# Storing the last two result tiles whole instead of in halves and quarters

## The chip, the cores and the metric

One core of a Trainium2 chip runs the program. The metric is the device time of one execution in microseconds (us), as the median over executions. A profile gives one execution in detail; its span is some 2 us shorter than that execution's time. "Tile" here is 64 of the 1024 matrices of the result, 1 MB (1,049 KB); there are 16, numbered 0 to 15, and the change concerns tiles 14 and 15.

## The reference

```python
a = np.random.randn(1024, 64, 64).astype(np.float32)
b = np.random.randn(1024, 64, 64).astype(np.float32)
return np.matmul(a, b).astype(np.float32)
```

33.5 MB are read and 16.8 MB written.

## The kernel before

The engines are named as in the profile: PE multiplies matrices, DVE and ACT are the vector and the scalar engine, POOL is the general one, and SP here issues transfers and waits for them. SBUF and PSUM are memories on the chip; the transfers themselves run on 16 DMA engines, fed by queues.

For each tile, `a` is transposed and spread into block-diagonal weights, `b` is cast to bf16, the matmuls fill PSUM, and ACT and DVE copy ("evacuate") the result into an SBUF tile `o_sb`. From there POOL's DMA queue stores it. The parts that matter:

```python
o_v = out.rearrange("(t gh x) (mo w) n -> t (x mo) gh (w n)", gh=8, x=8, w=4)
...
    o_sb = o_pool.tile([128, 8, 2, 2, 64], fp32, name="o_sb")

    def put(lo, n):                      # store n of the 8 parts, from lo on
        nc.gpsimd.dma_start(
            out=o_v[t, :, lo : lo + n, :],
            in_=o_sb[:, lo : lo + n].rearrange("p gh j wl n -> p (gh j wl n)"),
        )
...  # matmuls and evacuations; the last tile is evacuated in quarters, by ACT and DVE in turn
    if last:
        held[t] = [lambda q=q: put(2 * q, 2) for q in range(4)]
    else:
        whole = t < n_t - 2
        held[t] = [lambda q=q: put(q, 8 if whole else 4) for q in ([0] if whole else [0, 4])]
...
for t in range(n_t):
    ...
    multiply(t)
    ...
    if t >= HOLD - 1:                    # HOLD = 2: the store of t is issued after multiply(t + 1)
        store(t - HOLD + 1)
for t in range(n_t - HOLD + 1, n_t):
    store(t)
```

Each partition holds 8 KB of a tile, and by `o_v` they go to eight pieces of 1 KB in the output, 128 KB apart (`gh` steps over 8 matrices of 16 KB). A store waits only for the copies that fill its part of `o_sb`, so a half or quarter can be issued before the tile is complete. That is what the pieces are for.

Of the kernel before, what the change touches and what calls it, by code (L numbers as in the profile page):

```python
# [13 lines left out]
def kernel(  # L14
# [19 lines left out]
    n_t, n_s = B // 64, B // 128  # L34
# [27 lines left out]
    held = {}  # L62
# [90 lines left out]
    def multiply(t):  # L153
        at_bd = bd_tiles[t % N_BD][:].rearrange("p j g wl h mo -> p j g (wl h mo)")
        at_bd = at_bd.bitcast(bf16).rearrange("p j g (c u) -> p j g c u", u=2)
        b_bf = bbf_tiles.pop(t)
        last = t == n_t - 1
        o_sb = o_pool.tile([128, 8, 2, 2, 64], fp32, name="o_sb")

        def put(lo, n):  # L160
# [5 lines that stand above are left out]
        def evacuate(o_ps, gh, n, copies):  # L166

            for par in range(2):
                for wl in range(2):
                    src = o_ps[64 * wl : 64 * wl + 64, :, par, :, :]  # L170
                    dst = o_sb[64 * par : 64 * par + 64, gh : gh + n, :, wl, :]
                    copies[2 * par + wl](dst, src)  # L172

        for half in range(2):
            if not last:
                o_ps = o_psum.tile([128, 4, 2, 2, 64], fp32, name="o_ps")
            for g8 in range(8):
                if last and g8 % 4 == 0:
                    o_ps = t_psum.tile([128, 2, 2, 2, 64], fp32, name="at_ps")
                g = 8 * half + g8  # L180
                gl = (g8 % 4 if last else g8) // 2
                for j in range(2):
                    for u in range(2):
                        nc.tensor.matmul(  # L184
                            o_ps[:, gl, g % 2, j, :],
                            at_bd[:, j, g, :, u],
                            b_bf[:, g, 64 * u : 64 * u + 64],
                            start=(u == 0),
                            stop=(u == 1),
                        )  # L190
                if last and g8 % 4 == 3:
                    copy = nc.scalar.copy if g8 == 3 else nc.vector.tensor_copy
                    evacuate(o_ps, g // 4 * 2, 2, [copy] * 4)
            if not last:
                copies = [nc.scalar.copy] * 4
                if half and t % 2:
                    copies[2:] = [nc.vector.tensor_copy] * 2
                evacuate(o_ps, 4 * half, 4, copies)
        if last:
            held[t] = [lambda q=q: put(2 * q, 2) for q in range(4)]  # L200
        else:
            whole = t < n_t - 2
            held[t] = [lambda q=q: put(q, 8 if whole else 4) for q in ([0] if whole else [0, 4])]

    with tc.manual_schedule():
        load_first_a()
# [18 lines left out]
        for t in range(n_t):  # L225
            s, half = t // 2, t % 2
            if t + 1 < n_t:
                spread(t + 1)
                cast(t + 1)
            if t + B_AHEAD < n_t:  # L230
                load_b(t + B_AHEAD)
            if half == 0 and 0 < s < n_s - 1 - A_AHEAD:
                load_a(s + 1 + A_AHEAD)
            if half == 0 and 0 < s < n_s - 1:
                transpose(s + 1, 1)
            multiply(t)
            if t == 0:
                regroup(1)
                load_a(A_AHEAD)
                load_a(A_AHEAD + 1)  # L240
                transpose(1, 0)
                transpose(1, 1)
            elif t == 1:
                regroup(2)
            elif half == 0 and s + 2 < n_s:
                regroup(s + 2)
            if half == 1 and s + 2 < n_s:
                transpose(s + 2, 0)
            if t >= HOLD - 1:
                store(t - HOLD + 1)  # L250
# [32 lines left out]
```

## Time and profile before

| | before |
|---|---|
| time, median of 3 | 135.43 us (135.34 to 135.49) |
| profiled span | 133.8 us |
| last result copy ends | 121.4 us |
| last store issued / landed | 122.4 / 132.3 us |

The result stores on the page, by size (count, KB each, median us from issue to landing):

```profile
out_dram<-o_sb POOLq DMA_DIRECT2D x14, 1024.0 KB, 23.6
out_dram<-o_sb POOLq DMA_DIRECT2D x2, 512.0 KB, 11.4
out_dram<-o_sb POOLq DMA_DIRECT2D x4, 256.0 KB, 10.1
```

At the end the time to landing hardly depends on the size: a quarter tile takes 10.1 us, a half 11.4, and tile 13, stored whole, 12.7. (The 23.6 us of the whole tiles is a median over the entire kernel.) Such a time is mostly waiting in the queue.

### The profile page before, as it was taken

How to read it: one execution, taken by the hardware profiler on the slowest of the kernel's cores; microseconds unless marked ns; L12 is line 12 of the kernel's file. 1: busy time of each engine (PE TensorE's matmuls, PEld its weight loads, DVE VectorE, ACT ScalarE, POOL GpSimd, SP SyncE). 2: the span in 40 equal slices, each digit the busy share in tenths (PEclk: the TensorE clock that was granted, in tenths of full speed). 3: DMA queues.
4: the chain of work that ended last, by engine and by line, in shares of the span. 5: the costliest groups of instructions: out<-in, count | busy, mean ns of one | idle time of the engine just before them, and what ended most of it. 6: DMA issues, size and time to landing. Idle time of an engine off the chain costs nothing.

```text
span 133.8 us, 2832 instructions
## 1 busy us (share of the span) xinstructions
PE 65.7 (49%) x1152; PEld 62.7 (47%) x1152; DVE 94.6 (71%) x120; ACT 87.7 (66%) x161; POOL 38.5 (29%) x49
## 2 busy tenths in 40 slices
PE   0007307970077463749919744991876376640000
PEld 0007207970077353649909744991866266630000
DVE  5930499108997059999999999899959989992000
ACT  3225424998038996758998985899793987992000
POOL 8991000420091080334124042003301220637000
PEclk9999999999559999555996896589677775797555
DMA  3999999999999999999999999999999999999991
GB/s 75 376 331 311 306 315 311 307 301 309 306 307 382 366 312 309 388 397 397 317 304 352 399 392 377 314 307 364 398 385 391 392 401 398 404 388 353 338 334 42
DMA packets 17485, 45.01 MB, mean 336 GB/s; under 512 B 1088, under 2 KB 1088, under 8 KB 17472
## 3 DMA queue, kind: packets, MB, share of 16 engines
q0 software_dynamic: 7440, 22.28, 54.8%
q1 hardware_dynamic: 5520, 13.11, 27.0%
q10 hardware_dynamic: 4512, 9.44, 18.6%
q8 instruction: 9, 0.15, 0.4%
q14 instruction: 4, 0.03, 0.1%
HBM read 33.55 MB, written 16.78 MB: 376 GB/s over the span
## 4 chain that ended last, share of the span: by engine, by line
DMA 35%; SPq 27%; DVE 15%; issue 6%; ACT 3%; POOL 3%; PE 3%; POOLq 1%; DVEq 0%; ACTq 0%
SPq L72 22%; DMA a_raw<-in_a_dram 18%; DMA b_sb<-in_b_dram 17%; DVE at_bd L128 8%; DVE b_bf L139 5%; SPq L91 3%; POOL out_dram L161 3%; PE o_ps L184 3%; ACT o_sb L172 2%; DVE o_sb L172 1%; SPq L85 1%; ACT b_bf L146 1%; DVE a_bf L106 1%; DVE a_bf L103 1%; POOLq L278 1%
## 5 line engine op out<-in xcount | busy, mean ns | idle before, releaser
L172 ACT COPY o_sb<-o_ps 64x512 f32<-64x512 f32 x106 | 61.6, 581 | 14.3 <-PE o_ps L184 13.0
L184 PEld LDWEIGHTS <-at_bd 128*128 128x128 bf16 x1024 | 41.6, 111 | 34.9 <-DVE b_bf L139 22.4
L184 PE MATMUL o_ps<-b_bf,at_bd 128*128 128x64 bf16 x960 | 41.9, 215 | 31.1 <-DVE b_bf L139 20.9
L128 DVE COPY at_bd<-at_sb 32x1024 f32<-32x1024 f32 x64 | 46.0, 719 | 13.4 <-ACT at_sb L118 11.6
L161 POOL DMA_DIRECT2D out_dram<-o_sb x20 | 20.6, 1031 | 58.1 <-ACT o_sb L172 21.4
L115 PE MATMUL at_ps<-identity,a_bf 128*128 128x128 f32 x128 | 23.4, 360 | 20.6 <-ACT a_bf L100 11.0
L115 PEld LDWEIGHTS at_ps<-identity,a_bf 128*128 128x128 f32 x128 | 21.6, 196 | 20.8 <-issue 19.3
L118 ACT COPY at_sb<-at_ps 128x512 f32<-128x512 f32 x32 | 16.9, 596 | 8.2 <-PE at_ps L115 8.0
L68 POOL DMA_DIRECT2D a_sb<-in_a_dram x21 | 13.9, 673 | 25.9 <-DVE a_bf L103 19.9
L139 DVE CAST b_bf<-b_sb 128x2048 bf16<-128x2048 f32 x14 | 17.4, 1245 | 2.9 <-DMA b_sb<-in_b_dram 2.6
L172 DVE COPY o_sb<-o_ps 64x512 f32<-64x512 f32 x14 | 9.7, 690 | 0.6 <-ACT o_sb L172 0.3
L106 DVE CAST a_bf<-a_raw 128x1024 bf16<-128x1024 f32 x7 | 5.5, 792 | 5.7 <-DMA a_raw<-in_a_dram 5.7
L103 DVE COPY a_bf<-a_sb 128x3072 bf16<-128x3072 bf16 x7 | 7.0, 1006 | 0.0
L100 ACT CAST a_bf<-o_sb 128x1024 bf16<-128x1024 f32 x2 | 2.1, 1044 | 5.0 <-DMA o_sb<-in_a_dram 5.0
L139 ACT CAST b_bf<-b_sb 128x2048 bf16<-128x2048 f32 x1 | 1.9, 1898 | 3.8 <-DMA b_sb<-in_b_dram 3.8
L100 DVE CAST a_bf<-o_sb 128x1024 bf16<-128x1024 f32 x2 | 2.8, 1380 | 1.9 <-DMA o_sb<-in_a_dram 1.9
L212 DVE MEMSET at_bd<- 128x4096 f32 x1 | 3.5, 3472 | 0.8 <-issue 0.8
L172 DVE COPY o_sb<-at_ps 64x256 f32<-64x256 f32 x8 | 3.4, 422 | 0.3 <-PE at_ps L184 0.2
L172 ACT COPY o_sb<-at_ps 64x256 f32<-64x256 f32 x8 | 2.9, 367 | 0.1
L209 ACT ACT_TABLE_LOAD x1 | 1.3, 1283 | 2.3 <-issue 2.3
L184 PE MATMUL at_ps<-b_bf,at_bd 128*128 128x64 bf16 x64 | 2.0, 193 | 1.2 <-DVE at_bd L128 1.2
L217 POOL MEMSET at_bd<- 128x2048 f32 x1 | 1.8, 1849 | 0.0
(12 smaller groups left out, 5.5 us busy)
## 6 DMA issues: line engine op xcount, KB each, us to landing
out_dram<-o_sb POOLq DMA_DIRECT2D x14, 1024.0 KB, 23.6
a_sb<-in_a_dram POOLq DMA_DIRECT2D x21, 256.0 KB, 17.4
a_raw<-in_a_dram SPq DMA_DIRECT2D x7, 512.0 KB, 24.2
o_sb<-in_a_dram ACTq DMA_DIRECT2D x2, 512.0 KB, 7.0
o_sb<-in_a_dram SPq DMA_DIRECT2D x2, 512.0 KB, 5.9
out_dram<-o_sb POOLq DMA_DIRECT2D x2, 512.0 KB, 11.4
out_dram<-o_sb POOLq DMA_DIRECT2D x4, 256.0 KB, 10.1
b_sb<-in_b_dram SPq DMA_DIRECT2D x8, 0.5 KB, 22.2
```

Of the source, the lines that this page charges most:

```text
L68: nc.gpsimd.dma_start(out=a_sb[:, h, :, :].rearrange("p v k -> p (v k)"), in_=a_v[s, h])
L72: nc.sync.dma_start(out=a_raw[:].rearrange("p v k -> p (v k)"), in_=a_v[s, 3])
L100: copy(a_bf[:, :, h, :], a_sb[h].rearrange("p (v k) -> p v k", v=16))
L103: nc.vector.tensor_copy(a_bf[:, :, 0:3, :], cast_sb[:].rearrange("p h v k -> p v h k"))
L106: nc.vector.tensor_copy(a_bf[:, :, 3, :], raw[:])
L115: nc.tensor.transpose(at_ps[:, vo, :], a_cols[:, 4 * vo + 2 * j + wl, :], identity[:])
L118: nc.scalar.copy(at_tiles[s][:, j, :, wl, :, :], at_ps[:].rearrange("p vo (g mp) -> p g mp vo", mp=4),)
L128: nc.vector.tensor_copy(bd[rows, :, :, :, h, :].rearrange("p j g wl mo -> p j (g wl) mo"), at_tiles[t // 2][rows, :, half, :, :, :].rearrange(
L139: (nc.vector.tensor_copy if t else nc.scalar.copy)(b_bf[:], b_sb[:])
L161: nc.gpsimd.dma_start(out=o_v[t, :, lo : lo + n, :], in_=o_sb[:, lo : lo + n].rearrange("p gh j wl n -> p (gh j wl n)"),)
L172: copies[2 * par + wl](dst, src)
L184: nc.tensor.matmul(o_ps[:, gl, g % 2, j, :], at_bd[:, j, g, :, u], b_bf[:, g, 64 * u : 64 * u + 64], start=(u == 0), stop=(u == 1),)
```

## The change

It makes the code simpler: one store for every tile, four DMA issues fewer. The whole diff:

```diff
-        if last:
-            held[t] = [lambda q=q: put(2 * q, 2) for q in range(4)]
-        else:
-            whole = t < n_t - 2
-            held[t] = [lambda q=q: put(q, 8 if whole else 4) for q in ([0] if whole else [0, 4])]
+        held[t] = [lambda: put(0, 8)]
```

## The prediction

> **What bounds the kernel now.** The change touches only the last two result tiles, so the question is what sets the end of the span. I read the page's DMA rows first, then a table of windows over the end, then every result store with its landing, then the last instructions in order of time, and last who waits in the DMA queue's own sequencer (SP).
>
> The page's 40 slices (3.34 us each), for DMA share and for GB/s:
>
> ```profile
> DMA  3999999999999999999999999999999999999991
> GB/s 75 376 331 311 306 315 311 307 301 309 306 307 382 366 312 309 388 397 397 317 304 352 399 392 377 314 307 364 398 385 391 392 401 398 404 388 353 338 334 42
> ```
>
> Apart from the first and last slice the DMA engines are never under nine tenths busy, while on the same page the busiest compute engine, DVE, has 71% of the span. The transfers are the bound: first loads and stores together, at the end stores alone. The windows over the end (after the window's length come busy time and count for PE, PEld, DVE, ACT and POOL, then PE clock, DMA share, GB/s):
>
> ```profile
> 115.00:118.00 3.00, 1.83 (x59) 1.67 (x57) 2.72 (x5) 2.93 (x6) 1.10 (x2) 0.93 1.03 406
> 118.00:121.60 3.60, 0.49 (x17) 0.37 (x13) 2.97 (x8) 3.25 (x9) 2.18 (x3) 1.00 1.01 366
> 121.60:125.00 3.40, 0.00 (x0) 0.00 (x0) 0.00 (x0) 0.00 (x0) 1.42 (x2) 0.59 1.01 349
> 125.00:128.00 3.00, 0.00 (x0) 0.00 (x0) 0.00 (x0) 0.00 (x0) 0.00 (x0) 0.50 1.02 347
> 128.00:130.00 2.00, 0.00 (x0) 0.00 (x0) 0.00 (x0) 0.00 (x0) 0.00 (x0) 0.50 0.96 338
> 130.00:131.00 1.00, 0.00 (x0) 0.00 (x0) 0.00 (x0) 0.00 (x0) 0.00 (x0) 0.50 0.56 213
> 131.00:132.00 1.00, 0.00 (x0) 0.00 (x0) 0.00 (x0) 0.00 (x0) 0.00 (x0) 0.50 0.10 41
> ```
>
> Compute is over by 121.6 us; the DMA engines stay full until 130 us. So some 8 us of finished, queued stores drain after the last result copy. The last engine instructions, in order of time (start, length, engine, line, operation, count, idle before and its releaser):
>
> ```profile
> 116.23 0.92 POOL L161 DMA_DIRECT2D out_dram<-o_sb  x1 [1.05 <-ACT o_sb L172]
> ...
> 117.59 3.49 DVE L172 COPY o_sb<-at_ps 64x256 f32<-64x256 f32 x8 [0.22 <-PE at_ps L184]
> 118.34 3.03 ACT L172 COPY o_sb<-at_ps 64x256 f32<-64x256 f32 x8
> 118.61 0.75 POOL L161 DMA_DIRECT2D out_dram<-o_sb  x1 [1.46 <-ACT o_sb L172]
> 120.14 2.96 POOL L161 DMA_DIRECT2D out_dram<-o_sb  x4 [0.77 <-ACT o_sb L172]
> ```
>
> These are the six issues that the change replaces: tile 14 in halves at 116.23 and 118.61, tile 15 in quarters from 120.14 to 123.10. The reader should not take the end of the chain of waits (123.1 us) for the end of the kernel: that chain follows instructions, and 10.7 us of the span come after it. What they are is in the SP waits:
>
> ```profile
> SPq L278 <- DMA out_dram<-o_sb: 41.8, 3, 40.8
> ```
>
> SP sits at the program's last line until the result stores have landed. The end is therefore the landing of the last store plus the closing (the span ends at 133.8).
>
> The stores looked at one by one (issue start plus time to landing): tile 12 is issued at 108.71 and lands 15.2 us later, at 123.9; tile 13 at 113.83, 12.7 later, 126.5; the halves of tile 14 at 116.23 + 11.9 = 128.1 and 118.61 + 11.0 = 129.6; the quarters of tile 15 at 120.14 + 10.2 = 130.3, about 131.0, 121.67 + 10.0 = 131.7 and 122.38 + 9.9 = 132.3. Ten microseconds from issue to landing for 256 KB is queueing, not transfer.
>
> **What the Trainium skill says.** (1) "Perfetto Trace Analysis", section on the per-instruction lifecycle: the data movement of a DMA falls outside the reported window of its instruction. The trace agrees: a quarter's issue shows 0.71 us, its landing is 10 us away; so I use landings. (2) "DMA: Bandwidth & Descriptors", "Queues, rings and completion order": on each DMA engine descriptors are consumed in ring order. The section says it of the SP and ACT queues; for the POOL queue the landings above, in order of issue, agree. (3) The same page, "Measured (HBM→SBUF, 128 partitions, SWDGE, issued from GpSimd)": 64 KB reach 138 GB/s and 1 MB 341 GB/s, and it advises to batch to 1 MiB. That would make quarters poor. The trace does not agree for queued stores: the quarters land about 0.65 us apart, (132.3 - 130.3) / 3 = 0.67, which is 262 KB / 0.67 us = 390 GB/s. (4) The same page, "Anatomy of one DMA — SWDGE (gpsimd) path": about 2 us fixed per DMA, mostly completion latency. The 0.67 us between landings shows that it overlaps with the next transfer here.
>
> **The change part by part.** Nothing else moves: the order of instructions on PE, DVE, ACT and SP is unchanged, and POOL has 45 rows instead of 49.
>
> Tile 14. Removed: an issue of 0.92 us and one of 0.75 us. Added: one whole issue; the whole ones just before took 0.90 and 1.35 us. Moved: the first half (0.52 MB) is offered at 118.6 instead of 116.2, 2.4 us later, since the store must now wait for the last ACT copy of the tile, which already released the second half. Is this on the path? What is still to be moved at 118.6 is the sum of rate times length of the windows: 3.0 x 366 + 3.4 x 349 + 3 x 347 + 2 x 338 + 213 + 41 = 1098 + 1187 + 1041 + 676 + 254 = 4256 KB, and a tile is 1049 KB: 4.06 tiles, that is tiles 12 to 15 entire. Ahead of tile 14 lie two tiles, 2.1 MB, or 2.1 MB / 355 GB/s = 5.9 us of work. The issue takes at most 1.35 us. The delay is hidden with over 4 us to spare: cost 0.
>
> Tile 15. Removed: four issues, 2.96 us from 120.14 to 123.10. Added: one of 0.9 to 1.35 us, which can start when the last copy ends: ACT at 118.34 + 3.03 = 121.37 (DVE at 121.08), plus the 0.3 us seen between copy and issue (118.32 to 118.61), so 121.65, done by 122.6 to 123.0. The first quarter is offered 1.5 us later, the last no later than before. Still to be moved at 121.6: 4256 - 1098 = 3158 KB = 3.01 tiles, so tiles 13 and 14 lie ahead of it, some 6 us. Cost 0.
>
> The end. The same bytes go through the same 16 engines, which have no gap. Four completions fewer per engine: at 0.67 us a quarter against 1049 KB / 347 GB/s = 3.0 us a tile, a quarter of which is 0.76, I see no surcharge to win back; I put 0.1 us on it. Sum: 0 + 0 - 0.1 us, 135.43 to about 135.3.
>
> **The rivals.** (a) The delay shows. If my reading of the backlog is wrong, the worst is a tile 15 that finds the queues empty: 121.65 + 1.35 issue + 3.0 transfer + about 2 us of completion (the skill's figure, an estimate) = 128.0, still 4.3 us before today's last landing of 132.3. So even a wrong backlog does not lengthen the kernel by this way; only a slower transfer of whole tiles would. (b) Engine imbalance. The drop from full to empty takes 130 to 132 us, so engines differ by some 2 us; the leading ones reach tile 14 and 15 earlier than the mean. 5.9 us of work less 2 is still more than the delay, and an idle leader would not lengthen the laggard. (c) A gain: the rate falls from 406 GB/s before 118 us to about 347 after it, near the time at which halves and quarters are first queued. If small stores cause this, whole ones could move 11 us at 400 instead of 347: 11 x (1 - 347/400) = 1.5 us saved, 134.0 us. Against it: by the landings, what moves from 118 to 126 is mostly tiles 12 and 13, which are whole already. I give it about one in ten. (d) POOL: it is 29% busy, its last issue ends about where it did, and nothing else waits for it; no bound.
>
> **Range and chances.** The three runs before span 0.15 us, so noise is small. The middle is 135.3. Half of rival (c) gives about 134.5 as the low end; 0.6 us for something in the tail that I can't see gives 135.9. A change of 2% is 2.7 us, nearly twice the whole gain of (c) and, for a loss, as much as nearly a whole tile's transfer. Faster by over 2%: 0.02; within 2%: 0.96; slower: 0.02.
>
> **What would show it.** In the changed profile: one issue for tile 14 at about 118.6 and one for tile 15 at about 121.65; DMA share near 1 in every window until 130; landings of tile 14 near 129.6 and tile 15 near 132.2; compute ending unchanged at 121.4. Rival (c) would show as GB/s staying near 400 between 118 and 128 and the last landing near 131. I am wrong if a window between 118 and 129 shows a DMA share well under 1 (starved engines), or if whole tiles take clearly over 3 us each to land at the end.

## The result, and the profile after

The kernel after takes 135.44 us (median of 4, 135.23 to 135.56), beside 135.38 us for the kernel before on the same chip. The ratio is 1.0001, with a 95% interval of 0.9984 to 1.0019. Ratios here and below are the mean time of one kernel's runs over that of the other's of the same rounds, so not quite the ratio of the medians quoted.

The two DMA rows of its page hardly differ from those before (40 slices; DMA share in tenths, then GB/s):

```profile
DMA  3999999999999999999999999999999999999991
GB/s 72 373 330 309 309 315 311 308 303 305 307 307 379 371 297 316 391 394 398 315 308 351 403 384 379 314 309 361 395 391 389 393 398 398 408 388 361 343 340 69
```

The windows over the end, in the same columns as in the prediction:

```profile
115.00:118.00 3.00, 1.58 (x52) 1.46 (x50) 2.54 (x5) 2.94 (x6) 0.63 (x1) 0.99 1.02 403
118.00:121.60 3.60, 0.94 (x33) 0.82 (x29) 3.38 (x8) 3.48 (x10) 0.89 (x1) 1.00 1.04 378
121.60:125.00 3.40, 0.00 (x0) 0.00 (x0) 0.00 (x0) 0.06 (x1) 0.89 (x1) 0.54 1.00 345
125.00:128.00 3.00, 0.00 (x0) 0.00 (x0) 0.00 (x0) 0.00 (x0) 0.00 (x0) 0.50 1.01 345
128.00:130.00 2.00, 0.00 (x0) 0.00 (x0) 0.00 (x0) 0.00 (x0) 0.00 (x0) 0.50 0.95 338
```

The DMA share stays near 1 up to 130 us although the stores come later. The rate falls from 403 to 345 GB/s just as before, now with no small store in the queue. The last instructions in order of time:

```profile
118.05 3.47 DVE L172 COPY o_sb<-at_ps 64x256 f32<-64x256 f32 x8 [0.41 <-PE at_ps L184]
118.65 3.01 ACT L172 COPY o_sb<-at_ps 64x256 f32<-64x256 f32 x8
118.92 0.89 POOL L161 DMA_DIRECT2D out_dram<-o_sb  x1 [3.29 <-ACT o_sb L172]
122.06 0.89 POOL L161 DMA_DIRECT2D out_dram<-o_sb  x1 [2.26 <-ACT o_sb L172]
```

Two issues stand where six stood. Tile 14 is offered whole at 118.92 and takes 10.5 us to land, at 129.4; tile 15 at 122.06, and takes 10.1, landing at 132.1 to 132.2. Before, the last halves and quarters landed at 129.6 and 132.3.

### The profile page after: what moved, and what is told of

It reads as the page before. It is cut to its first block, busy times and chain, and to the rows that moved or that the text cites. A ratio compares the mean times of both kernels' runs of the same rounds, so it can differ in the third digit from the quotient of the medians.

```text
span 133.4 us, 2824 instructions
## 1 busy us (share of the span) xinstructions
PE 64.3 (48%) x1152; PEld 60.6 (45%) x1152; DVE 94.9 (71%) x120; ACT 87.7 (66%) x161; POOL 35.6 (27%) x45
## 4 chain that ended last, share of the span: by engine, by line
DMA 34%; DVE 19%; SPq 16%; ACT 9%; PE 7%; issue 6%; POOLq 1%; ACTq 1%; DVEq 0%
DMA b_sb<-in_b_dram 34%; SPq L72 13%; DVE at_bd L128 8%; ACT o_sb L172 7%; DVE o_sb L172 5%; PE o_ps L184 3%; DVE b_bf L139 3%; PE at_ps L115 3%; SPq L91 2%; ACT at_sb L118 2%; DVE a_bf L106 1%; DVE a_bf L103 1%; SPq L85 1%; PE at_ps L184 1%; POOLq L274 1%
## 5 line engine op out<-in xcount | busy, mean ns | idle before, releaser
L184 PEld LDWEIGHTS <-at_bd 128*128 128x128 bf16 x1024 | 40.3, 110 | 37.6 <-DVE b_bf L139 23.6
L184 PE MATMUL o_ps<-b_bf,at_bd 128*128 128x64 bf16 x960 | 40.6, 212 | 32.8 <-DVE b_bf L139 20.8
L161 POOL DMA_DIRECT2D out_dram<-o_sb x16 | 18.5, 1155 | 60.5 <-ACT o_sb L172 24.8
L115 PE MATMUL at_ps<-identity,a_bf 128*128 128x128 f32 x128 | 22.9, 354 | 20.4 <-ACT a_bf L100 11.2
L115 PEld LDWEIGHTS at_ps<-identity,a_bf 128*128 128x128 f32 x128 | 20.7, 189 | 20.6 <-issue 19.9
L68 POOL DMA_DIRECT2D a_sb<-in_a_dram x21 | 13.0, 634 | 26.2 <-DVE a_bf L103 19.7
L106 DVE CAST a_bf<-a_raw 128x1024 bf16<-128x1024 f32 x7 | 6.3, 907 | 5.7 <-DMA a_raw<-in_a_dram 5.7
```

What stands on the lines that cost most here:

```text
L68: nc.gpsimd.dma_start(out=a_sb[:, h, :, :].rearrange("p v k -> p (v k)"), in_=a_v[s, h])
L106: nc.vector.tensor_copy(a_bf[:, :, 3, :], raw[:])
L115: nc.tensor.transpose(at_ps[:, vo, :], a_cols[:, 4 * vo + 2 * j + wl, :], identity[:])
L161: nc.gpsimd.dma_start(out=o_v[t, :, lo : lo + n, :], in_=o_sb[:, lo : lo + n].rearrange("p gh j wl n -> p (gh j wl n)"),)
L184: nc.tensor.matmul(o_ps[:, gl, g % 2, j, :], at_bd[:, j, g, :, u], b_bf[:, g, 64 * u : 64 * u + 64], start=(u == 0), stop=(u == 1),)
```

## The experiments

The theory: two tiles of queued stores lie ahead of each of the last two, so the moment at which these are issued doesn't matter until the queue is nearly dry. Rivals: (1) the issue of the last store is on the path and something else gave its cost back; (2) pieces and whole stores cost the same in themselves, backlog or not; (3) small stores cost the DMA engines extra, and the fewer stores paid for the later issue. Where an expectation below counts 2 us for the completion of a store, that is the Trainium skill's figure which the prediction names ("DMA: Bandwidth & Descriptors", "Anatomy of one DMA — SWDGE (gpsimd) path"), and so an estimate.

### Issuing the last store later: three, five and seven memsets ahead of it

```diff
+    scratch = consts.tile([128, 2048], fp32)
...
+        for _ in range(3):               # 5 and 7 in the other two
+            nc.gpsimd.memset(scratch[:], 0.0)
         for t in range(n_t - HOLD + 1, n_t):
             store(t)
```

A memset here is POOL writing zeros to a scratch tile; it only takes time (five of them 9.28 us). All three are edits of the kernel after, and compute the right result.

> Three memsets of about 1.85 us each stand on POOL between the issue of tile 14 and that of tile 15, so tile 15 should be issued near 125.4 us instead of 122.1. Backlog theory: tiles 13 and 14 keep the DMA engines full until about 127, so the time stays at 135.4 (0 to +0.4 us). Rival, the issue of the last store is on the path: +3.4 us, 138.8.

> Five memsets: tile 15 issued near 129.1 us. Backlog theory: past the knee; the engines run dry before it, and it lands about 5.9 us after its issue (0.9 issue, 3.0 transfer, 2 completion, an estimate), near 135.0 instead of 132: +2 to +3.5 us, 137.4 to 138.9, with a window of low DMA share between 128 and 131. Rival (full cost): +7.0 us, 142.4.

> Seven memsets: tile 15 issued near 132.8 us. Backlog theory: slope 1 past the knee, so 3.7 us more than with five: +5.5 to +7.5 us, 141 to 143, and the knee, found by drawing the line back, near an issue at 126 to 127 us. Rival (full cost): +10.8 us, 146.2.

Measured, beside 135.34 us for the kernel before in the same rounds:

| memsets | tile 15 issued at | time | ratio to before (95%) |
|---|---|---|---|
| none (the kernel after, its own rounds) | 122.06 us | 135.44 us | 1.0001 (0.9984 to 1.0019) |
| 3 | 125.02 us | 135.08 us | 0.9984 (0.9969 to 0.9999) |
| 5 | 128.56 us | 136.77 us | 1.0114 (1.0099 to 1.0129) |
| 7 | 132.58 us | 140.73 us | 1.0393 (1.0373 to 1.0412) |

The POOL timeline of the kernel with five memsets, and then two windows of it:

```profile
118.46 0.89 POOL L162 DMA_DIRECT2D out_dram<-o_sb  x1 [3.31 <-ACT o_sb L173]
119.34 9.28 POOL L249 MEMSET scratch<- 128x2048 f32 x5
128.56 0.89 POOL L162 DMA_DIRECT2D out_dram<-o_sb  x1
```

```profile
125.00:128.00 3.00, 0.00 (x0) 0.00 (x0) 0.00 (x0) 0.00 (x0) 2.94 (x2) 0.50 0.72 264
128.00:130.00 2.00, 0.00 (x0) 0.00 (x0) 0.00 (x0) 0.00 (x0) 1.45 (x2) 0.50 0.02 8
```

Here the engines do run dry: a share of 0.02 while the store is being issued. Between five and seven memsets the issue moves by 132.58 - 128.56 = 4.02 us and the time by 140.73 - 136.77 = 3.96 us, one for one. Drawn back to the time of before, 136.77 - 135.34 = 1.43 us earlier, the knee (the issue time beyond which the kernel gets longer) is at 128.56 - 1.43 = 127.1 us. The kernel after issues tile 15 at 122.06, so it has 5.0 us to spare. The rival "on the path" expected 138.8 us with three memsets; measured were 135.08, not longer at all. It is refuted, and the third rival with it: a later issue has no cost here that fewer stores could pay for.

The slope came out as expected, the sizes narrowly missed. With five memsets the cost was 1.4 us where 2 to 3.5 were expected: the store was issued 0.5 us earlier than I had put it (128.56 for 129.1), and a lone whole tile took 5.1 us from issue to landing and not 5.9. With seven it was 5.4 us where 5.5 to 7.5 were expected, and the knee lies just above the expected 126 to 127.

### Taking the backlog away: tiles 8 to 13 not stored

```diff
-            if t >= HOLD - 1:
+            if t >= HOLD - 1 and not 8 <= t - HOLD + 1 < n_t - 2:
                 store(t - HOLD + 1)
```

The edit is made once in the kernel before (pieces) and once in the kernel after (whole). The result is wrong, since six tiles are missing.

> Wrong result on purpose: tiles 8 to 13 are never stored, so the last two tiles meet empty DMA queues; tile 14 in halves and tile 15 in quarters as before the change. With compute ending near 121.4 and the last quarter issued by 123.1, the last landing should come near 125 to 126, so about 128 to 129 us in all (5 to 8 us less than with the backlog).

> The same with the last two tiles stored whole. Backlog theory: pieces matter exactly where the queues are empty, so this one is slower than empty_pieces by 1 to 2.5 us (transfer of 1 MB after the issue at 122, about 3.0 us, instead of 0.7 us for a last quarter after an issue that ends at 123.1). Rival (whole and pieces cost the same by themselves, and the backlog has nothing to do with it): no difference, within 0.3 us.

With pieces: 130.39 us (129.43 to 130.54), ratio 0.9606 (0.9569 to 0.9642). Whole: 132.52 us (130.80 to 132.70), ratio 0.9750 (0.9688 to 0.9811). The runs of each scatter by more than a microsecond, but every whole one is slower than every one with pieces. The difference of the medians is 2.1 us, or 1.6%. POOL with pieces:

```profile
116.82 0.89 POOL L161 DMA_DIRECT2D out_dram<-o_sb  x1 [36.50 <-ACT o_sb L172]
119.22 0.75 POOL L161 DMA_DIRECT2D out_dram<-o_sb  x1 [1.52 <-ACT o_sb L172]
120.75 2.24 POOL L161 DMA_DIRECT2D out_dram<-o_sb  x3 [0.77 <-ACT o_sb L172]
123.16 0.72 POOL L161 DMA_DIRECT2D out_dram<-o_sb  x1 [0.17 <-issue]
```

and whole:

```profile
118.99 0.89 POOL L161 DMA_DIRECT2D out_dram<-o_sb  x1 [39.36 <-ACT o_sb L172]
123.16 0.89 POOL L161 DMA_DIRECT2D out_dram<-o_sb  x1 [3.29 <-issue]
```

The last issue starts at the same time, 123.16 us. What differs is how much it carries: the last quarter lands 3.3 us later, the whole tile 5.1 us later. That is 1.7 us of the 2.1; the rest is not accounted for. So the pieces do what they were made for, by some 2 us, when the queue is empty, and the rival "no difference by themselves" is refuted. Both absolute times were above the 128 to 129 us that I expected for the pieces: in these profiles the last copy ended at 122.6 to 122.9 instead of 121.4 us, and 2.1 to 2.3 us instead of 1.5 passed between the last landing and the end of the span.

### What a queued small store costs: tiles 8 to 15 in quarters, and in halves

```diff
-        held[t] = [lambda: put(0, 8)]
+        if t >= 8:
+            held[t] = [lambda q=q: put(2 * q, 2) for q in range(4)]   # halves: put(4 * q, 4), range(2)
+        else:
+            held[t] = [lambda: put(0, 8)]
```

> All tiles from 8 to 15 are stored in quarters: 32 stores where there were 8, 24 more. Backlog theory with no surcharge for a queued store: time unchanged, 135.4, within 0.7 us. If each extra store cost the DMA engines 0.1 us: +2.4 us, 137.8. If the fixed 2 us of a small DMA did not overlap: far above 150 us. A possible new wait: every eighth later store of the POOL queue waits for an earlier one to land, which holds at most eight quarters, 2 MB, in the queue; that would show as POOL idle before a store with a store's landing as releaser, at little cost so long as the DMA share stays near 1.

> Tiles 8 to 15 stored in halves, 8 stores more than whole. In the run with quarters the 24 extra stores cost 1.7 us and the rate fell to about 320 GB/s. If each queued store has a surcharge (1.7 / 24 = 0.07 us): +0.6 us, about 136.0. If instead the quarters lost because POOL's issuing (0.72 us for 262 KB) and the limit of eight stores in the queue kept the backlog short: halves leave a backlog of up to four tiles, so no loss, 135.4 within 0.3 us, and 395 to 405 GB/s between 110 and 118.

Quarters: 137.21 us beside 135.52, ratio 1.0119 (1.0102 to 1.0136), so 1.7 us more, where no change within 0.7 was expected. Halves: 135.45 us beside 135.52, ratio 0.9989 (0.9971 to 1.0007). Both results are right. The POOL timeline and two windows of the kernel with quarters:

```profile
110.05 0.72 POOL L161 DMA_DIRECT2D out_dram<-o_sb  x1 [4.45 <-DMA out_dram<-o_sb]
111.55 17.30 POOL L161 DMA_DIRECT2D out_dram<-o_sb  x24 [0.79 <-DMA out_dram<-o_sb]
```

```profile
115.00:118.00 3.00, 2.28 (x67) 2.12 (x65) 2.50 (x6) 2.93 (x6) 3.00 (x5) 0.86 1.01 350
125.00:128.00 3.00, 0.00 (x0) 0.00 (x0) 0.00 (x0) 0.00 (x0) 3.00 (x5) 0.50 1.01 321
```

A new wait appears, POOL waiting for an earlier store to land, and then POOL issues without a pause: 24 quarters of 262 KB in 17.30 us can offer at most 24 x 262 / 17.30 = 364 GB/s. The engines are recorded as busy all the same, but at 350 GB/s from 115 to 118 us, where the kernel after has 403, and at 321 from 125 to 128, where it has 345. A fixed surcharge per store, 1.7 / 24 = 0.07 us, would have cost the halves 0.6 us; their interval allows at most 0.0007 x 135.5 = 0.1 us, and they moved 401 and 406 GB/s in the windows from 110 to 118 us, as expected. So a queued half is free, and a steady flow of quarters is not.

The cause is only narrowed down. In both traces never more than eight stores are under way, and with halves POOL waits for a landing too (1.37 us before the issue at 113.98), at no cost. A lack of issued work should show as idle engines, and it doesn't. From 118 to 128 us POOL even offered more than was moved, 364 GB/s against 319 to 321, and the time to landing grew from 4.1 us (the quarter issued at 115.17) to 6.0 (126.71). So at the end neither POOL's pace nor the limit of eight held the rate down. Whether it was the size itself, or the issuing that went on beside the transfers, is open.

### Where the fall of the rate comes from: other addresses

The fall from 403 to 345 GB/s after 118 us, in both kernels, was the only sign of a possible gain. This run writes the same bytes of tiles 8 to 15 in whole stores to contiguous places, 8 KB for each partition, so the result is wrong.

```diff
-        held[t] = [lambda: put(0, 8)]
+        def put_plain():
+            nc.gpsimd.dma_start(
+                out=out[64 * t : 64 * t + 64].rearrange("r (c w) n -> (r c) (w n)", c=2),
+                in_=o_sb[:].rearrange("p gh j wl n -> p (gh j wl n)"),
+            )
+
+        held[t] = [put_plain] if t >= 8 else [lambda: put(0, 8)]
```

> Wrong result on purpose: tiles 8 to 15 are stored whole with each partition's 8 KB as one contiguous piece of the output instead of eight pieces of 1 KB, to see whether the fall of the rate from 400 to 345 GB/s after 118 us belongs to the pattern of addresses. If it does: near 400 to the end, 1.3 us faster, about 134. If the fall comes with stores alone, whatever their addresses: 345 after 118 and the time within 0.4 us of 135.4.

134.37 us beside 135.52, ratio 0.9912 (0.9898 to 0.9927). Its windows:

```profile
115.00:118.00 3.00, 2.20 (x65) 2.08 (x63) 2.50 (x6) 2.94 (x6) 0.29 (x1) 0.90 1.02 429
118.00:121.60 3.60, 0.70 (x24) 0.57 (x20) 3.17 (x8) 3.49 (x9) 0.53 (x1) 1.00 1.01 416
121.60:125.00 3.40, 0.00 (x0) 0.00 (x0) 0.00 (x0) 0.45 (x2) 0.53 (x1) 0.62 1.01 426
```

The fall is gone: 416 and 426 GB/s where the kernel after has 378 and 345. Before 118 us the gain is smaller, 429 against 403. So the fall needs the pattern of pieces in the output; the size of the stores, or stores as such, don't bring it. The last store lands at 130.2 us, 2 us earlier, of which the time shows 1.1 us, because the closing after it took 2.3 us this time. Two things stay open: whether the length of a piece (1 KB against 8) or the distance between pieces (128 KB) is at fault, and why the same pattern still moves at 403 before 118 us. The end of the compute isn't the reason: in the run with pieces and no backlog the same pattern moved 253 GB/s at a share of 0.74 from 118 to 121.6 us, so some 342 at full share, while DVE and ACT were still copying.

### The last stores from SP's queue

```diff
-            nc.gpsimd.dma_start(
+            (nc.sync if t >= n_t - 2 else nc.gpsimd).dma_start(      # n_t - 4 in the other
                 out=o_v[t, :, lo : lo + n, :],
```

> The last two tiles stored whole from SP's queue instead of POOL's. If the bytes and the 16 engines alone set the end, the time stays at 135.4 (within 0.5 us). If the fall of the rate from 400 to 347 GB/s after 118 us belongs to the POOL queue's own way of making descriptors, it would be up to 1.3 us faster, about 134.1, with GB/s near 400 to the end.

> Tiles 12 to 15 stored whole from SP's queue. With the last two there the time was 0.6 us shorter, at an unchanged rate. If the gain comes from the issue (SP starts a store sooner after the last copy than POOL) it stays at 0.6 us, about 134.8; if it comes from sharing each engine between two queues, four tiles on one queue lose it again, 135.4.

Two tiles: 134.75 us beside 135.34, ratio 0.9961 (0.9946 to 0.9977). Four tiles: 134.90 us beside 135.52, ratio 0.9951 (0.9936 to 0.9966). Both results are right, so these are a little better than the two kernels compared. With two tiles neither expectation fits: the gain is 0.6 us, and the rate falls nearly as before (357 and 349 GB/s from 121.6 to 128 us, where the kernel after has 345). The issues on SP come no earlier (119.08 and 123.3 us, in an execution whose compute ran later). What differs most is the very end. The window from 130 to 131 us of the kernel after, and then of the kernel with two tiles on SP:

```profile
130.00:131.00 1.00, 0.00 (x0) 0.00 (x0) 0.00 (x0) 0.00 (x0) 0.00 (x0) 0.50 0.59 229
```

```profile
130.00:131.00 1.00, 0.00 (x0) 0.00 (x0) 0.00 (x0) 0.00 (x0) 0.00 (x0) 0.50 0.40 140
```

Less is left for the engines that finish last, and the last store lands at 131.6 instead of 132.1 us. Four tiles keep the gain, which speaks against "sharing each engine between two queues". The number fits the other branch, a sooner issue, but with the backlog an issue even 3 us later cost nothing, so that isn't shown either; the reason was not isolated.

## Why the prediction was right

The prediction was 135.3 us, within 2%; measured were 135.44 us and a ratio of 1.0001.

- **What bounds the end.** Right: the time follows the landing of the last store, and an issue 3 us later still (three memsets) did not lengthen it. The last three tiles landed 2.7 us apart (126.7, 129.4, 132.1), so neither sign of being wrong appeared.
- **Tile 14, cost 0.** Right. Its first half was offered at 118.92 instead of 116.23, and the tile landed at 129.4 (forecast near 129.6).
- **Tile 15, cost 0.** Right in size too. From the 3.01 tiles left at 121.6 us I had "some 6 us" ahead of it, so a queue that lasts until 127.6; the delayed issues put the knee at 127.1. The tile landed at 132.1 to 132.2 (forecast 132.2). It was issued at 122.06 and not 121.65, mostly because the copies ended 0.3 us later in this execution.
- **The end, -0.1 us.** Not to be seen: the interval of the ratio is 0.5 us wide. That the sum came so near is no evidence for this term. Halves throughout cost nothing, which agrees with a surcharge near zero for them; for quarters nothing shows it (24 more cost 1.7 us).
- **The skill on small transfers.** I let three landing gaps of quarters, 390 GB/s, speak against it. That reading was wrong: those are the last engines finishing while others are already idle. From 130 to 132 us, when these quarters landed, the prediction's own windows count 254 KB moved (213 and 41 GB/s), not three quarters of 262 KB. In a steady flow of quarters the rate was 319 to 350 GB/s, and the kernel lost 1.2%. That the fixed 2 us overlap was right: 24 stores more cost 1.7 us, not 48.
- **Rival (a), the delay shows.** It was rightly set aside. The lone store was sized too long at 6.35 us from issue start to landing (1.35 + 3.0 + 2); with the queue dry it took 5.0 to 5.1. The bound holds all the more.
- **Rival (c), a gain of 1.5 us if small stores cause the fall of the rate.** Refuted by the result itself, since whole stores show the same fall, and the run with other addresses shows whose it is.

## What to carry to other kernels

In this kernel, cutting the last stores into pieces was worth some 2 us without a backlog and nothing with one. Before cutting elsewhere, add up what the DMA queues still hold when the last result is ready (rate times length of the windows to the end), and compare that with the delay in question. If the queue is the longer one, look at the rate at which it drains instead, which here depended on the pattern of pieces in the output.

## What the Trainium skill lacked or had wrong

- "DMA: Bandwidth & Descriptors", "Why small descriptors are slow (HBM only)": its example is a descriptor of 256 bytes, with a fixed overhead of 3 cycles on 8 per packet. If each piece is one, the same sum gives 3 on 32 for 1 KB, some 9% (an estimate). Here pieces of 1 KB, 128 KB apart, drained at 345 GB/s at the end, and 8 KB contiguous pieces of the same amount at 426, 23% more; from 115 to 118 us it was 403 against 429, 6%. No run separates length from distance.
- The same page, "Measured (HBM→SBUF, 128 partitions, SWDGE, issued from GpSimd)": the table doesn't say what a size costs when other stores are queued. Here halves of 512 KB were free (ratio 0.9989) and a steady flow of 256 KB quarters cost 1.2%, with rates of 319 to 350 GB/s, POOL issuing one every 0.72 us.
- The same page, "Anatomy of one DMA — SWDGE (gpsimd) path": its fit, 2.0 us plus bytes over 436 GB/s, gives an estimate of 4.4 us for a lone 1 MB store; it took 5.0 to 5.1 us from issue to landing here. At the 345 GB/s of this pattern the same sum gives 2.0 + 3.0 = 5.0.
- The same page, "Queues, rings and completion order": it tells the order of completion for the SP and ACT queues only, and no page tells in which order stores of POOL's queue land. Here the last eight of the kernel before landed in the order of their issue, from 123.9 to 132.3 us.
